# Index scores one by one with dense pieces between them, and two gate tiles moved ahead of the second forgetting pair, in a hybrid attention trunk

## The chip, the cores and the metric

The kernel runs on one core of one Trainium2 chip, in one launch. The metric is the device time of the launch in microseconds (us). Engines: PE is TensorE (matmuls), DVE is VectorE, ACT is ScalarE, POOL is GpSimd, SP is SyncE, which here issues DMAs.

## The reference

One layer of a decoder trunk on 512 tokens of width 1024, float32:

```python
x = x + token_mixer(rmsnorm(x, g1), ...)      # four causal token mixers A to D, gated, summed, @ w_out
x = x + conv_ffn(rmsnorm(x, g2), ...)         # gated MLP, width 2816, causal depthwise conv of width 3
return rmsnorm(x, g3)
```

`token_mixer` makes one projection of the normalised input and splits it into queries, keys and values of four mixers with four heads of 64 each: stick-breaking attention (S below), block-sparse attention with a T5 bias (M, "MoBA"), forgetting attention (F, "FoX") and D, attention over the 128 keys per query that an indexer selects. The indexer's score of query t and key s is a sum over 8 index heads of width 32, `sum_h w[t,h] * relu(q_idx[t,h] . k_idx[s])`, and the top 128 per row are kept. Stick-breaking needs, for each row, `log_sigmoid(-z)` and its reverse running sum, and weighs values with `exp(log_sigmoid(z) + that sum)`. Each mixer's output is multiplied with `w_branch`, gated with `sigmoid(xn @ w_gate)`, summed and multiplied with `w_out`.

## The kernel before, in words

All large products are made at about float32 precision by splitting each operand into a rounded part (hi) and a rest (lo) and adding three products (hi hi, hi lo, lo hi) in PSUM. A projection tile (128 outputs, 512 tokens, depth 1024) is thus 24 matmuls of 512 columns. `proj` (line 258) and `dense_steps` (line 114) hand them out in four pieces of six; the planner books 1.28 us for each (line 122). A values tile (VS, VM; `vgroup`, line 294) is 12 pieces of eight matmuls of 256 columns, booked at 0.85 us. After a tile's last piece its eviction follows: multiplication with the row factor on DVE (line 266), then copies and subtractions on ACT and DVE for the hi and lo parts. Each weight tile is loaded by SP (line 100), cast to hi on ACT (line 90) and subtracted to lo on POOL or DVE (line 91); three buffers of hi and lo serve all tiles in the order of the stream.

TensorE's order is written out by hand: it runs the program in the order in which the Python code emits it. The other engines' order is made by a scheduler. The mixer stage (lines 628 to 711) takes 16 heads in the order F0 F1, S0 S1, F2 F3, S2 S3, then M and D, one per "step" n = 0 to 15, and ends with steps 16 and 17. (F0q, F0k name the first forgetting *pair*, heads F0 and F1; F1q, F1k the second, heads F2 and F3; S0q to S1k in the same way.) In each step:

- `slot(n, 0, 1.5)` emits dense pieces until 1.5 us are booked; then the head's scores begin, in up to four parts (for softmax heads one block of 128 rows each, 128, 256, 384 and 512 columns wide; for S heads the matmuls `z` of four column blocks, two of them in the third part). After each part, index scores may follow (lines 703 and 704), then `slot(n, pos, ...)` with quotas of 0.5, 2, 0.5 and 1 us, then one more of 1 us (QUOTA, line 890).
- A slot first emits what falls due from earlier heads: for a softmax head, `turn` (transposes of the softmax, line 476) one step later and `pv` (line 494) two steps later, both at position 1; for an S head `weights` (line 537) one step later and `pv` two steps later, both at position 3 (LAG, line 892).
- `dense(us)` (line 609) takes the next tile of ORDER (line 885). If the tile's GATE (line 887) is a step not yet reached, it returns with nothing; it does not skip to a later tile. F1q opens in step 2, S1q in step 4, M0q in step 6. Two tiles are never in work at a time.

Index scores: 24 of them, for row blocks 3, 2 and 1 and eight heads each (line 636), in groups of three: one group after the last part of head 0, four groups in step 1, three in step 2 (IXN, line 893). Each (line 423) is one matmul of 512, 384 or 256 columns into a PSUM bank of its own, a relu on ACT and a multiply-add into the block's sum on DVE; the bank is free after that. Banks of this kind are six, shared with scores, transposes, `pv` and the z of S heads; projections have two more. When all index scores are out, DVE gets the rounds of the top-128 search (line 439), a few per slot.

The S head: after its z, ACT takes Abs (line 524), Exp (526) and Ln (527), DVE three additions (529), ACT a cast to `lh` (533), POOL the subtraction to `ll` (534). `weights` multiplies a triangle matrix with `lh` and then with `ll` (line 545), block by block, on top of z.

Of a gate tile (G0 to G7 for the first branch, H0 to H7 for the second) only the projection and one DVE multiplication are made in this stage.

Of the kernel before, what the change touches and what calls it, by code (L numbers as in the profile page):

```python
# [49 lines left out]
def trunk(ctx: ExitStack, tc: tile.TileContext, xt, wv0, wv, wp, wdk, wg, wb, wo, wu, wd,  # L50
# [79 lines left out]
    def bank(name, tag="a"):  # L130
        return psum.tile([P, S], F32, name=name, tag=tag, bufs=6 if tag == "a" else 2)
# [22 lines left out]
    stream.append((wdk, (KT, 100), V))  # L154
    order = ORDER.split()
    pidx = {"ix0": 0, "ix1": 1, "F0q": 2, "F0k": 3, "F1q": 4, "F1k": 5, "M0q": 6, "M0k": 7, "M1q": 8, "M1k": 9,
# [21 lines left out]
    with ExitStack() as ph:  # L178
# [228 lines left out]
        def bias_head(h):  # L407
            e = pp.tile([P, S], F32, name=f"e{h}", tag="e", bufs=3)
            r = bdram[h // 4][h % 4].rearrange("p y -> (p y)")
            SP.dma_start(e, r[127:127 + P * 639].rearrange("(p y) -> p y", y=639)[:, :S])  # L410
            return e
# [11 lines left out]
        def index_score(i, h):  # L423
            n = P * (i + 1)
            if h == 0:
                isc[i] = pp.tile([P, n], F32, name=f"isc{i}")
            t = isc[i]
            ps = bank(f"ip{i}{h}")[:, :n]
            T.matmul(ps, iq[h][:, i * P:(i + 1) * P], ixk[:, :n], start=True, stop=True)
            A.activation(ps, ps, AF.Relu)  # L430
            if h == 0:
                V.tensor_scalar(out=t, in0=ps, scalar1=ixw[:, i, 0:1], scalar2=None, op0=OP.mult)
            else:
                V.scalar_tensor_tensor(out=t, in0=ps, scalar=ixw[:, i, h:h + 1], in1=t, op0=OP.mult, op1=OP.add)
            if h == 7:
                G.affine_select(out=t[:, i * P:], in_=t[:, i * P:], pattern=[[-1, P]], base=0, channel_multiplier=1,
                                compare_op=OP.is_ge, fill=INADM)
# [171 lines left out]
        def dense(us):  # L609

            while us > 0 and (state["gen"] is not None or state["i"] < len(order)):
                if state["gen"] is None:
                    key = order[state["i"]]
                    if GATE.get(key, -1) > step[0]:
                        return
                    state["gen"] = dense_item(key)
                try:
                    us -= next(state["gen"])
                except StopIteration:
                    finished.add(order[state["i"]])  # L620
                    state["gen"] = None
                    state["i"] += 1

        def require(key):
            while key not in finished:
                dense(0.1)
# [30 lines left out]
        def topk(n):  # L657
            nonlocal done_topk
            for _ in range(n):
                if not done_topk and next(tk, "end") == "end":  # L660
                    done_topk = True
# [6 lines left out]
        def slot(n, pos, us):  # L668
            for st, nm in due.pop((n, pos), ()):
                if nm in "SM":  # L670
                    require("V" + nm)
                st()
            dense(us)
            if not idx:
                tkc[0] += TKS[min(n, 15)]
                while tkc[0] >= 1:
                    topk(1)
                    tkc[0] -= 1
# [3 lines left out]
        while due or n < len(heads):  # L682
            step[0] = n
            if n in BCOPY:
                i = BCOPY.index(n)
                with tc.issue_after(kdma[0].ins):
                    SP.dma_start(bdram[i], brd[4 * i:4 * i + 4].rearrange("p (o y) -> p o y", o=1).to_broadcast([4, P, 640]))
            for h in EBIAS.get(n, ()):
                with tc.issue_after(kdma[0].ins):
                    ebias[h] = bias_head(h)  # L690
            slot(n, 0, QUOTA[0])
            if n < len(heads):
                pr, nm, stages = heads[n]
                require(pr + "q")
                if nm == "D":
                    topk(100)
                else:
                    require(pr + "k")
                parts = stages[0]()
            for pos in range(1, 5):  # L700
                if n < len(heads):
                    next(parts, None)
                    for _ in range(min(len(idx), IXN[min(4 * n + pos - 1, 4)])):
                        index_score(*idx.pop(0))
                slot(n, pos, QUOTA[pos])
            if n < len(heads):
                for _ in parts:
                    pass
            slot(n, 5, QUOTA[5])
            n += 1  # L710
# [137 lines left out]
    for f in range(KT):  # L848
# [11 lines left out]
        else:  # L860
# [21 lines left out]
NV0 = 328  # L882
DCH = ((0, 8), (8, 8), (16, 6))

ORDER = ("ix0 ix1 F0q F0k S0q S0k VS F1q F1k G0 S1q S1k G1 M0q M0k VM M1q M1k G2 G3 D0q G4 G5 D1q G6 G7 "
         "H0 H1 H2 H3 H4 H5 H6 H7")
GATE = {"F1q": 2, "S1q": 4, "M0q": 6, "VM": 7, "M1q": 8, "D0q": 10, "D1q": 12, "H0": 10, "H4": 12}

# [2 lines left out]

LAG = [((1, 1), (2, 1)), ((1, 3), (2, 3))]
IXN = [0, 0, 0, 3, 3]
TKS = [1.2] * 16
EBIAS = {6: (0, 1), 8: (2,), 10: (3,), 11: (4, 5), 12: (6,), 14: (7,)}
BCOPY = (2, 5)
# [96 lines left out]
```

## Time and profile before

| what | value |
|---|---|
| time, median of 3 runs | 857.58 us (857.57 to 859.62) |
| the profiled execution's own time | 857.41 us |
| its span, first to last instruction | 855.6 us |
| PE busy | 837.3 us, 98% of the span |
| DVE busy | 538.1 us, 63% |
| ACT busy | 398.8 us, 47% |
| POOL busy | 164.6 us, 19% |
| mean granted TensorE clock | 0.996 of full |

The times of the sections below are us from the span's start. Profiled durations are to be set against 857.41 us; 1.8 us of it lie outside the span. An instruction's row has its start, its duration, engine, line, operation, what it writes and reads, its shape, how many follow one another, and in brackets the engine's idle time before it with what ended it. Matmuls overlap: one starts before the one ahead of it has ended, so the distance between two starts tells what a matmul costs.

### The profile page before, as it was taken

What the parts mean: (1) busy time and instruction counts of PE and PEld (TensorE: products, weight loads), DVE (VectorE), ACT (ScalarE), POOL (GpSimd) and SP (SyncE); (2) the same over time, 40 slices, a digit from 0 to 9 for tenths busy, and PEclk for the clock granted to TensorE, in tenths of its full rate; (3) what the DMA queues carried; (4) which work ended last, traced back from release to release, by engine and by line L of the source; (5) the groups of instructions that cost most, each with busy time, mean ns of one, the idle gap of its engine ahead of it and who ended that gap; (6) DMA issues with size and microseconds to landing.
All of it is one profiled execution on the core that took longest, in us unless ns stands there. A gap on an engine that the chain in (4) does not pass through costs nothing.

```text
span 855.6 us, 10625 instructions
## 1 busy us (share of the span) xinstructions
PE 837.3 (98%) x4019; PEld 702.2 (82%) x4019; DVE 538.1 (63%) x931; ACT 398.8 (47%) x612; POOL 164.6 (19%) x131
## 2 busy tenths in 40 slices
PE   8999999999999999999999999999999999999995
PEld 7778887888888888888888888888888888888885
DVE  5947899996453468455554477777777777333234
ACT  6556785664554843232344454444444444232231
POOL 1244575377568300000001200000000000000000
PEclk9999999999999999999999999999999999999998
DMA  6567334326332243232223223333333333333322
GB/s 227 167 163 178 100 132 108 87 58 189 90 120 74 75 130 117 74 103 96 77 74 107 89 98 98 99 99 99 98 99 99 98 97 91 90 93 93 90 65 98
DMA packets 31667, 90.68 MB, mean 106 GB/s; under 512 B 3384, under 2 KB 8376, under 8 KB 31616
## 3 DMA queue, kind: packets, MB, share of 16 engines
q1 hardware_dynamic: 30240, 88.62, 34.3%
q10 hardware_dynamic: 1376, 1.38, 0.5%
q8 instruction: 31, 0.51, 0.2%
q14 instruction: 20, 0.16, 0.1%
HBM read 83.78 MB, written 5.82 MB: 105 GB/s over the span
## 4 chain that ended last, share of the span: by engine, by line
PE 80%; DVE 1%; POOL 0%; ACT 0%; issue 0%; DVEq 0%; POOLq 0%
PE u L120 28%; PE dg L120 19%; PE dn L833 14%; PE o L120 5%; PE b L120 5%; PE vpsVM L303 1%; PE dM1q L120 1%; PE dM1k L120 1%; PE zb L545 1%; PE dD1q L120 1%; PE dD0q L120 1%; PE ptD L484 1%; PE ptM L484 1%; PE dM0q L120 0%; PE oD L500 0%; PE oM L500 0%
## 5 line engine op out<-in xcount | busy, mean ns | idle before, releaser
L90 ACT CAST wh<-wr 128x1024 fp32r<-128x1024 f32 (+1 forms) x129 | 133.7, 1039 | 153.8 <-PE dn L833 70.4
L91 DVE TENSOR_TENSOR wl<-wr,wh 128x1024 fp32r<-128x1024 f32 (+2 forms) x97 | 116.3, 1200 | 138.6 <-ACT wh L90 63.6
L120 PE MATMUL u<-xhi,wh 128*128 128x512 f32 x352 | 87.5, 390 | 0.0
L91 POOL TENSOR_TENSOR wl<-wr,wh 128x1024 fp32r<-128x1024 f32 x32 | 77.0, 2408 | 52.9 <-PE dix L120 15.3
L120 PE MATMUL u<-xlo,wh 128*128 128x512 f32 x352 | 87.1, 389 | 0.0
L120 PE MATMUL u<-xhi,wl 128*128 128x512 f32 x352 | 87.1, 389 | 0.0
L809 DVE SCALAR_TENSOR_TENSOR cv<-h,cvp,cv 128x511 f32<-128x511 f32 x88 | 66.0, 751 | 26.2 <-ACT cv L807 24.6
L120 PEld LDWEIGHTS u<-xhi,wh 128*128 128x128 f32 x352 | 66.1, 188 | 14.1 <-issue 0.5
L120 PEld LDWEIGHTS u<-xlo,wh 128*128 128x128 f32 x352 | 66.1, 188 | 13.7
L120 PEld LDWEIGHTS u<-xhi,wl 128*128 128x128 f32 x352 | 66.1, 188 | 13.7
L807 ACT ACTIVATE cv<-h,cvp 128x512 f32<-128x512 f32 x44 | 35.9, 815 | 79.8 <-DVE h L805 79.8
L833 PE MATMUL dn<-mh,wh 128*128 128x512 f32 (+1 forms) x198 | 72.9, 368 | 0.0
L833 PE MATMUL dn<-ml,wh 128*128 128x512 f32 (+1 forms) x198 | 72.3, 365 | 0.0
L833 PE MATMUL dn<-mh,wl 128*128 128x512 f32 (+1 forms) x198 | 72.3, 365 | 0.0
L120 PE MATMUL dg<-xlo,wh 128*128 128x512 f32 x256 | 66.1, 392 | 0.0
L120 PE MATMUL dg<-xhi,wh 128*128 128x512 f32 x256 | 64.9, 390 | 0.0
L120 PE MATMUL dg<-xhi,wl 128*128 128x512 f32 x256 | 64.3, 390 | 0.0
L120 PEld LDWEIGHTS dg<-xhi,wl 128*128 128x128 f32 x256 | 47.7, 188 | 9.8
L120 PEld LDWEIGHTS dg<-xhi,wh 128*128 128x128 f32 x256 | 47.8, 188 | 9.4
L120 PEld LDWEIGHTS dg<-xlo,wh 128*128 128x128 f32 x256 | 47.4, 188 | 9.5
L781 POOL TENSOR_TENSOR rstd<-rstd,sqo 128x512 f32<-128x512 f32 x7 | 9.1, 1302 | 187.1 <-ACT sqo L780 187.1
L833 PEld LDWEIGHTS dn<-ml,wh 128*128 128x128 f32 x198 | 37.3, 188 | 6.2
(430 smaller groups left out, 1453.0 us busy)
## 6 DMA issues: line engine op xcount, KB each, us to landing
wr<-in_wu SPq DMA_DIRECT2D x44, 512.0 KB
wr<-in_wg SPq DMA_DIRECT2D x32, 512.0 KB
wr<-in_wp SPq DMA_DIRECT2D x16, 512.0 KB
wr<-in_wd SPq DMA_DIRECT2D x16, 512.0 KB
wbr<-in_wb SPq DMA_DIRECT2D x8, 512.0 KB
wr<-in_wo SPq DMA_DIRECT2D x8, 512.0 KB
wr<-in_wd SPq DMA_DIRECT2D x8, 384.0 KB
bdram<-brd SPq DMA_DIRECT2D x2, 1280.0 KB
```

Source lines behind the costliest of these rows:

```text
L90: A.copy(hi, raw)
L91: eng.tensor_tensor(out=lo, in0=raw, in1=fr(hi), op=OP.subtract)
L120: T.matmul(o, a[:, k], b(k), start=(n == 0), stop=(n == len(todo) - 1))
L303: T.matmul(ps, a[:, k, ts_], b, start=(m == 0), stop=(m == 3 * KT - 1))
L484: T.transpose(pt[:, (i - j) * P:(i - j + 1) * P], z[:, QOFF[i] + P * j:QOFF[i] + P * (j + 1)], ident)
L545: T.matmul(zs[j][:, P * (j2 - j):n], trir if j2 == j else negr, x[:, KOFF[j2]:KOFF[j2] + n2], start=False, stop=(j2 == NB - 1 and x is ll) ...
L781: G.tensor_tensor(out=acc, in0=acc, in1=sq, op=OP.add)
L807: A.activation(c, h, AF.Identity, scale=cvp[:, i, 2:3], bias=cvp[:, i, 3:4])
L809: V.scalar_tensor_tensor(out=c[:, x:], in0=h[:, :S - x], scalar=cvp[:, i, 2 - x:3 - x], in1=c[:, x:], op0=OP.mult, op1=OP.add)
L833: T.matmul(o, a, b[:, k, cs], start=(n == 0 and m == 0), stop=(n == ND - 1 and m == 2))
```

## The change

After each index score, `dense(0.4)` emits one piece of dense work (a piece is the least it can emit), so a group of three scores has a piece behind each; and G0 and G1, which stood behind F1k and behind S1k, stand ahead of F1q in the order. The gates are as before. G0 and G1 have none.

```diff
                     for _ in range(min(len(idx), IXN[min(4 * n + pos - 1, 4)])):
                         index_score(*idx.pop(0))
+                        dense(IXD)
                 slot(n, pos, QUOTA[pos])
...
-ORDER = ("ix0 ix1 F0q F0k S0q S0k VS F1q F1k G0 S1q S1k G1 M0q M0k VM M1q M1k G2 G3 D0q G4 G5 D1q G6 G7 "
+ORDER = ("ix0 ix1 F0q F0k S0q S0k VS G0 G1 F1q F1k S1q S1k M0q M0k VM M1q M1k G2 G3 D0q G4 G5 D1q G6 G7 "
          "H0 H1 H2 H3 H4 H5 H6 H7")
...
 IXN = [0, 0, 0, 3, 3]
+IXD = 0.4
```

## Rows read from the trace of the kernel before

**Rows 1.** The page: engines' busy time, and POOL's costliest group (busy, mean ns).

```profile
PE 837.3 (98%) x4019; PEld 702.2 (82%) x4019; DVE 538.1 (63%) x931; ACT 398.8 (47%) x612; POOL 164.6 (19%) x131
...
L91 POOL TENSOR_TENSOR wl<-wr,wh 128x1024 fp32r<-128x1024 f32 x32 | 77.0, 2408 | 52.9 <-PE dix L120 15.3
```

**Rows 2.** Windows: length; PE, PEld, DVE, ACT, POOL busy (x); PEclk, DMA, GB/s.

```profile
350.00:450.00 100.00, 100.00 (x443) 82.81 (x442) 55.41 (x69) 34.00 (x42) 0.00 (x0) 1.00 0.29 88
```

**Rows 3.** PE's timeline, around the index scores of steps 0 and 1.

```profile
69.96 0.85 PE L429 MATMUL ip<-ixk,iq 128*128 128x512 f32 x3
70.66 1.11 PE L303 MATMUL vpsVS<-wh,xlo 128*128 128x256 f32 x8
...
79.61 0.28 PE L464 MATMUL sF<-kF0k,qF0q 128*128 128x256 f32 x1
...
86.56 2.02 PE L120 MATMUL dF1q<-xhi,wh 128*128 128x512 f32 x8
```

**Rows 4.** Waits of PE: us in total, times, longest.

```profile
PE ip L429 <- DVE stF L467: 0.6, 1, 0.6
...
PE ip L429 <- DVE isc L434: 0.4, 2, 0.2
```

**Rows 5.** Timeline of all engines, from the last z of S0 to its weights.

```profile
98.39 0.27 PE L521 MATMUL zb<-mskr,idr 128*128 128x128 f32 x1
...
99.88 0.49 ACT L524 ACTIVATE a<-zb 128x384 f32<-128x384 f32 x1
...
101.09 1.29 ACT L526 ACTIVATE a<-a 128x1280 f32<-128x1280 f32 x1
...
103.19 1.38 ACT L527 ACTIVATE a<-a,one 128x1280 f32<-128x1280 f32 x1
...
104.61 1.62 DVE L529 SCALAR_TENSOR_TENSOR a<-zb,a 128x512 f32<-128x512 f32 x3 [0.71 <-ACT a L527]
...
105.71 0.39 PE L519 MATMUL zb<-qS0q,kS0k 128*128 128x512 f32 x1
...
106.23 0.45 PE L499 MATMUL oF<-phF,vvF 128*128 128x512 f32 x1
106.32 1.26 ACT L533 CAST lh<-a 128x1280 fp32r<-128x1280 f32 x1 [1.28 <-DVE a L529]
...
107.50 1.14 PE L120 MATMUL dg<-xlo,wh 128*128 128x512 f32 x4
107.66 2.97 POOL L534 TENSOR_TENSOR ll<-a,lh 128x1280 fp32r<-128x1280 f32 x1 [1.85 <-ACT lh L533]
...
111.85 0.45 PE L545 MATMUL zb<-lh,trir 128*128 128x512 f32 x1
...
112.49 0.44 PE L545 MATMUL zb<-ll,trir 128*128 128x512 f32 x1
```

**Rows 6.** PE's timeline: F2's softmax and transposes, the last z of S2, VM.

```profile
128.37 1.07 PE L120 MATMUL dS1k<-xlo,wh 128*128 128x512 f32 x4
...
134.92 0.98 PE L484 MATMUL ptF<-cst,zF 128*128 128x128 f32 x7 [0.42 <-POOL zF L472]
...
152.63 0.27 PE L521 MATMUL zb<-mskr,idr 128*128 128x128 f32 x1
...
163.50 1.22 PE L303 MATMUL vpsVM<-wh,xhi 128*128 128x256 f32 x8 [1.30 <-DVE vvM L211]
```

**Rows 7.** POOL's timeline: the last block of F0's softmax, S2's subtraction.

```profile
72.94 1.04 POOL L472 TENSOR_TENSOR zF<-zF,stF 128x512 f32<-128x512 f32 x1 [2.05 <-DVE stF L471]
...
159.76 2.94 POOL L534 TENSOR_TENSOR ll<-a,lh 128x1280 fp32r<-128x1280 f32 x1
```

**Rows 8.** PE's timeline: its first matmuls (warming up) and its last.

```profile
1.32 4.16 PE L200 MATMUL wps<-warm 128*128 128x512 f32 x9 [1.32 <-POOL warm L186]
...
846.34 0.70 PE L840 MATMUL msf<-sqe,cst 128*128 128x256 f32 x2 [0.96 <-ACT sqe L872]
```

**Rows 9.** Windows behind the last matmul, same columns as rows 2.

```profile
848.00:850.00 2.00, 0.00 (x0) 0.00 (x0) 1.86 (x4) 0.00 (x1) 0.00 (x0) 0.59 0.00 0
```

## The prediction

> **What bounds the kernel now.** The page first: TensorE (PE) is busy for 98% of the span [rows 1]. The windows say where that is certain: between 350 and 450 us PE is busy for all 100.00 us, at the full clock [rows 2], and in the chain of waits the later stages are PE's matmuls one behind the other. Whatever is lost ahead of that stretch moves the end by as much, and whatever is saved likewise. So only the token mixer, up to about 200 us, has room, and there the PE timeline is to be read, by the starts of its instructions, because its order is written out by hand and nothing overtakes.
>
> The place that the change aims at is the index scores. Three scores of 512 columns that wait for nothing stand 0.70 us apart from the next work, 0.233 us each [rows 3]. From the scores of FOX (forgetting attention) head F1, block 1, at 79.61 to the first matmul of F1q at 86.56 PE takes 6.95 us [rows 3]. The work in it, priced by columns from that 0.70: block 1 of F1 about 0.25, three scores of up to 512 columns 0.70, a VS piece 1.1 [rows 3], block 2 about 0.35, three scores of 384 columns 0.5, block 3 about 0.45, three more scores 0.5; sum 3.85. So 3.1 us are stall: scores wait for PSUM banks, which come free when VectorE (DVE) has added the earlier ones. The list of waits puts only 0.6 and 0.4 us on these scores [rows 4]; it counts gaps between modelled ends, and the starts say 3.1. I take the starts. The Trainium skill, Trainium Kernel Development and Optimization, section Performance Expectations, warns that matmul busy time judges badly because matmuls are pipelined; this stretch agrees (1.0 us of gaps, 3.1 us by starts). By the gaps alone the gain below would be 2.1 us smaller.
>
> **The change, part by part.** I follow the planner's loops by hand with the old and the new numbers. No matmul, transfer or eviction is added or removed: the 24 scores stay, the projections stay. What changes is which work stands between which on PE.
>
> First, after each score one piece of dense work follows. In step 0 the three scores get VS pieces between them. In step 1, G0 and G1 stand next in the order, ungated, so of their eight pieces six go behind the step's first six scores and two to its quotas, and both tiles are done halfway through the step; then F1q is gated (it opens in step 2), and six scores of 384 columns come bare again, with blocks 2 and 3 of F1 among them. In step 2, F1q and F1k go wholly between the scores. Then S1q is gated until step 4.
>
> The gain: up to 3.1 us of stall goes, since a piece of six matmuls, 6 x 0.233 = 1.4 us, is longer than the DVE addition that a score waits for. The six bare scores may still wait for a bank; I leave 0.6 us there, the longer of the two waits on them [rows 4]. Gain 2.5, between 1.0 (six of the stretch's nine scores are bare, and keep 6/9 of the 3.1) and 3.1.
>
> What moves with a tile: G0 and G1 bring their weight load on SP's queue, a cast on ScalarE (ACT) and a subtraction on GpSimd (POOL), ahead of those of F1q and F1k. The tiles keep their places in the stream one for one, so a load, a cast and a subtraction of the same size stand where the others stood. I cost that at nothing; the cover is the PE work between a tile's split and its use, now more of it. Were it gone, one POOL subtraction of 2.4 us [rows 1] would show.
>
> The price: what is taken ahead is missing later. Step 3 now has no dense work at all (it had G0), nor has step 5 (it had G1), and the last three pieces of F1k no longer stand behind the scores in step 2. G0 was 24 matmuls, 24 x 0.233 = 5.6 us.
>
> Step 3 holds "weights S0", which needs the whole chain of stick-breaking head S0. Its last score matmul starts at 98.39 and ends at 98.66; then ACT takes Abs 0.49, Exp 1.29, Ln 1.38, DVE 1.62, ACT's cast 1.26, POOL's subtraction 2.97, which ends at 110.63 [rows 5]. That is 12.0 us from the last score, 9.0 us of bare work. Head S2 takes 152.90 to 162.70, 9.8 us [rows 6, 7]. Before the change PE came to the weights at 111.85 [rows 5], just when they were ready: F1k's pieces and G0 were the cover. Afterwards only this stands between: three scores of 256 columns 0.4 (half the columns of the 0.70), z of S1 block 0 0.52, pv of F1 1.27 [rows 5], the three narrower z blocks about 0.4 and 0.6, together 3.2; and the first four matmuls of the weights, which need only lh, 0.64 [rows 5]. Cover 3.9. The chain in the new place: F1q's copies, which held back Abs until 99.88 though the scores ended at 98.66 [rows 5], are done long before; that takes 1.2 off the 12.0. F1k's casts, S1's Abs and the index relus stay. I take 10.8. Stall 10.8 - 3.9 = 6.9; between 5.1 (9.0 of bare work) and 8.1 (12.0 as now).
>
> While PE waits so long its clock may fall. At the tail it is at full speed until the last matmuls at 846.34 and then falls: the mean of 848 to 850 is 0.59, on the way from 2.4 to 1.2 GHz [rows 8, 9]. Ahead of the fall PE did only these two matmuls, after a gap of 0.96 [rows 8]. At the start the nine warming matmuls take 4.16 us [rows 8], 0.46 each against 0.233: about 4 us at the low level. Waking up again costs half of that, 2.0 us. Within the mixer the clock stayed at full through a gap of 1.30 [rows 6], so those rows say nothing of 6.9 us. I take the fall, +2.0. The Trainium skill, TensorE: Matmul & The Clock Gate, section Why this matters for your kernels, says that idle gaps between bursts of matmuls bring the clock back to half rate; no stretch of this trace ahead of the tail shows it. By that rule the sum holds the 2.0, by the mixer's rows alone it would be 2.0 lower.
>
> Step 5 has "turn F2" without G1 ahead. It needs the last block of F2's softmax. F0's chain took from 69.96 to 73.98, 4.0 us [rows 3, 7]; F2's own took from 128.37 to 134.92, 6.55 us [rows 6], and PE paid 0.42 of it. New cover: S1k's last two pieces 2.8, the first block of F3 and three transposes about 0.3; 3.1. Stall 0.9 to 3.45; I take 2.0, between, because in F2's chain POOL also did a weight split, which need not fall there again. Minus 0.4: +1.6. Behind it, pv of S1 and F3's blocks come quicker than ph and pl leave their banks: +0.4, between nothing and 1.6 (DVE's pass over one head's blocks, 1.62 [rows 5], in the way).
>
> Given back later: DVE has top-k rounds in its backlog, for which PE waits, as at 163.50, 1.30 us [rows 6]. When PE stalls, DVE catches up: -0.8, between nothing and -1.3, the whole of that wait.
>
> Sum: -2.5 + 6.9 + 2.0 + 1.6 + 0.4 - 0.8 = +7.6, on the profiled execution's 857.4 us (span 855.6, 1.8 outside it), which stands 0.2 under the median of 857.58. That gives 865.0.
>
> **The rivals.**
>
> The clock stays up: everything else as above, +5.6, 863.0. For it speaks that the four lh matmuls and step 3's scores break up the wait; against it the fall at the tail, with two matmuls just ahead. Chance 0.22.
>
> The clock falls twice, or the step 5 wait is as long as F2's chain: +2.0 and more on the sum, 867 to 870. It is decided in step 5, by whether PE's wait there, too, is enough for a fall. Chance 0.13.
>
> A draw: the chain of S0 runs near its bare 9.0 us since ACT and DVE have less to do (stall 5.1), the clock stays, step 5 costs 0.5, the scores give 3.1 and DVE gives back 1.3: 5.1 + 0.5 - 3.1 - 1.3 = +1.2, 858.6. Chance 0.15.
>
> The other side, faster: the weights of S0 are not waited for, and the scores' 2.5 stay: 854.9. This decides at one point: S0's chain, last score to ll, would have to be under 3.9 + 2.5 = 6.4 us. Against it stands the sum of its rows, 9.0 us in series on three engines; for it only that the records of a busy mixer may overstate what an emptier one needs. Chance 0.08.
>
> That the change doesn't do what it says, because weights for G0 come too late, would leave PE waiting in step 1 and add to the loss; the splits have 5 us and more of PE work ahead of them, and I give it nothing of its own.
>
> **How the numbers follow.** Forecast 0.42, clock stays 0.22, worse 0.13, draw 0.15, faster 0.08. A measurement of this kernel tells some 0.3%, 2.6 us, from no change: slower 0.77, same 0.15, faster 0.08. The point is the forecast's. The range leaves out the faster case, the draw's lower half and the far end of the worse one: 858.6 to 869.5.
>
> **What would show it.** In the changed profile: the 512-column scores with a piece behind each, 1.6 us apart, and no wait on isc until the bare six. PE's longest wait then is at the second half of "weights S0" (line 545), released by POOL's ll (line 534), ACT's lh just before; some 3 us for each. A granted clock under 1.00 in the window of that wait and just behind it. A wait of "turn F2" (line 484) for POOL's z, about 2 us. From step 10 on the order is the same, and the shift against before is constant. I am wrong if weights S0 follows S1's last z block within 2 us, or if ll is done under 7 us after S0's last score; and if the clock reads 1.00 throughout, that term falls.

## The result, and the profile after

The changed kernel takes 871.67 us (median of 5 runs, 870.20 to 873.01) against 857.58 of the kernel before (5 runs beside it): ratio 1.0158, 95% interval [1.0142, 1.0174], so slower by 14 us. The forecast was 865.0 with a range of 858.6 to 869.5: the direction held, the size did not.

The page after, to stand beside [rows 1]; PEclk is the granted clock of TensorE in 40 slices, in tenths, 9 being 90% or more:

```profile
span 868.6 us, 10634 instructions
...
PE 840.5 (97%) x4019; PEld 706.2 (81%) x4019; DVE 537.9 (62%) x931; ACT 400.5 (46%) x612; POOL 164.6 (19%) x131
...
PEclk9999989999999999999999999999999999999998
```

The span grew by 13.0 us (855.6 before). Counts are the same; PE's busy time rose by 3.2 us because the same matmuls ran slower in a few places, and the rest is idle time. The list of PE's waits says what ended it (total, times, longest; the list that [rows 4] show for the kernel before):

```profile
PE ip L429 <- DVE plF L488: 4.5, 1, 4.5
PE zb L519 <- DVE oTf L503: 3.5, 2, 3.3
PE ptF L484 <- POOL zF L472: 1.9, 2, 1.2
PE zb L519 <- DVE isc L434: 1.3, 1, 1.3
...
PE oS L499 <- DVE stF L467: 1.2, 1, 1.2
...
PE vpsVM L303 <- DVE vvM L211: 0.9, 1, 0.9
```

The longest wait is one that the prediction did not have: an index score waits 4.5 us. Before asking why, it helps to see where in the mixer the time went. Six anchors on PE's timeline cut it into five stages; in the kernel before the last three are these rows (the first three are the 69.96 of [rows 3] and the 98.39 and 112.49 of [rows 5]):

```profile
114.63 0.67 PE L120 MATMUL dS1q<-xhi,wh 128*128 128x512 f32 x2
...
140.81 0.39 PE L120 MATMUL dM0q<-xhi,wh 128*128 128x512 f32 x1
...
207.17 0.39 PE L120 MATMUL dD0q<-xhi,wh 128*128 128x512 f32 x1
```

and in the changed kernel:

```profile
69.68 0.39 PE L429 MATMUL ip<-ixk,iq 128*128 128x512 f32 x1
...
116.77 0.28 PE L521 MATMUL zb<-mskr,idr 128*128 128x128 f32 x1
...
128.09 0.80 PE L545 MATMUL zb<-ll,trir 128*128 128x512 f32 x1 [0.32 <-POOL ll L534]
...
131.79 1.60 PE L120 MATMUL dS1q<-xhi,wh 128*128 128x512 f32 x6
...
154.12 2.00 PE L120 MATMUL dM0q<-xhi,wh 128*128 128x512 f32 x8
...
219.78 0.61 PE L120 MATMUL dD0q<-xhi,wh 128*128 128x512 f32 x2
```

A stage's distance minus the matmuls in it, at 0.227 us for 512 columns (443 of them fall into the 100 us of [rows 2]) and less for narrower ones (0.12 for 256, the step between their starts at full clock), is what PE lost there. Stages: A from the first index score to the last z of S0, B on to the first matmul that needs ll, C on to S1q, D on to M0q, E on to D0q. In us:

| kernel | A | B | C | D | E |
|---|---|---|---|---|---|
| before | 5.1 | 1.0 | 0.3 | 2.1 | 6.2 |
| changed | 8.8 | 7.7 | 1.9 | 3.7 | 5.5 |
| difference | +3.7 | +6.7 | +1.6 | +1.6 | -0.7 |

A is where the index scores stand (steps 0 to 2), B is step 3, D is step 5 at its end. The differences sum to 12.9 of the span's 13.0. The levels hang on the price of the transposes of 128 columns: they are counted at about 0.06 here, while their starts stand 0.11 us apart at full clock. At that price A, D and E are lower by about 0.8, 0.4 and 0.7 in every kernel, and the differences stay. Of A's +3.7, the forecast had said -2.5.

**Stage A.** ACT's timeline, between the scores of step 1:

```profile
83.27 0.58 ACT L430 ACTIVATE ip<-ip 128x512 f32<-128x512 f32 x1 [1.00 <-PE ip L429]
91.12 1.04 ACT L90 CAST wh<-wr 128x1024 fp32r<-128x1024 f32 x1 [7.27 <-DMA wr<-in_wp]
92.07 1.40 ACT L487 CAST phF<-ptF 128x512 fp32r<-128x512 f32 x4
93.34 0.62 ACT L430 ACTIVATE ip<-ip 128x512 f32<-128x512 f32 x1
```

ACT stands still for 7.27 us because the next instruction in its order is the cast of a weight tile (F1k's) that has not landed. Behind it stand turn F0's copies and the relu of the next score. PE does not need that tile until 107 us; it needs the bank that those copies empty:

```profile
87.83 1.07 PE L120 MATMUL dg<-xlo,wh 128*128 128x512 f32 x4
93.43 0.50 PE L429 MATMUL ip<-ixk,iq 128*128 128x512 f32 x1 [4.53 <-DVE plF L488]
93.77 1.80 PE L120 MATMUL dg<-xlo,wh 128*128 128x512 f32 x4
```

SP's queue says why the tile is late. The load was issued at 80.39, the copy of the bias rows (line 687, 1280 KB within DRAM) at 69.84, ahead of it in the same queue:

```profile
69.84 0.71 SPq L687 DMA_DIRECT2D bdram<-brd  x1
80.39 14.58 SPq L100 DMA_DIRECT2D wr<-in_wp  x3
```

(The second row runs together three loads, of which F1k's is the first.)

The DMA view of 74 to 92 us gives the time from issue to landing, 10.6 us:

```profile
wr<-in_wp SPq DMA_DIRECT2D x2, 512.0 KB, 10.6
```

In the kernel before that copy was issued at 70.57, the load of the tile in F1k's stream place only at 84.75, and its cast stood behind the copies of turn F1, at 94.11, with nothing waiting for it:

```profile
84.75 2.66 SPq L100 DMA_DIRECT2D wr<-in_wp  x2
```

```profile
94.11 1.05 ACT L90 CAST wh<-wr 128x1024 fp32r<-128x1024 f32 x1 [0.34 <-ACT phF L487]
```

When G0 and G1 are used up in step 1 (before the change in steps 3 and 5), the tile two places ahead in the stream is asked for earlier too, and its cast moves to the front of turn F0's copies.

**Stage B** went as forecast in size. PE's timeline, step 3:

```profile
119.20 0.50 PE L519 MATMUL zb<-qS0q,kS0k 128*128 128x512 f32 x1 [1.34 <-DVE isc L434]
...
125.05 0.58 PE L519 MATMUL zb<-qS0q,kS0k 128*128 128x256 f32 x1 [3.32 <-DVE oTf L503]
...
126.18 0.41 PE L521 MATMUL zb<-mskr,idr 128*128 128x128 f32 x1
126.39 0.73 PE L545 MATMUL zb<-lh,trir 128*128 128x512 f32 x1
```

and POOL's end of S0's chain:

```profile
125.11 2.93 POOL L534 TENSOR_TENSOR ll<-a,lh 128x1280 fp32r<-128x1280 f32 x1 [4.19 <-ACT lh L533]
```

From the start of S0's last z at 116.77 to the end of ll at 128.04 the chain takes 11.3 us (11.0 when counted from that matmul's end, as the forecast's 10.8 is), and the matmuls under it come to 3.6 (forecast 3.9). The loss is the difference; only its place is another. PE never gets to stand 6.9 us at weights S0, since the z blocks of S1 ahead of them wait first, for a bank of an index score and for the bank of pv F1, whose addition on DVE stands behind S0's own 1.62 us and a step of the top-128 search there.

**Stage C** is the clock. Windows (length; PE, PEld, DVE, ACT, POOL busy; PEclk, DMA share, GB/s):

```profile
94.00:97.00 3.00, 3.00 (x9) 2.33 (x8) 2.29 (x7) 2.25 (x5) 1.52 (x3) 0.50 0.36 94
...
125.00:128.00 3.00, 2.72 (x10) 2.43 (x10) 2.83 (x5) 1.36 (x3) 2.89 (x1) 0.50 0.26 102
128.00:131.00 3.00, 2.91 (x11) 2.82 (x12) 2.93 (x7) 2.27 (x3) 0.04 (x1) 0.50 0.29 108
```

So 1.2 GHz in two places, behind the gap of 4.53 us in step 1 and behind that of 3.32 in step 3 (0.50 is the lower of the clock's two levels). The prediction weighed the Trainium skill, TensorE: Matmul & The Clock Gate, section Why this matters for your kernels (idle gaps between bursts bring the clock back to half rate): the changed kernel's trace agrees, 0.50 after both gaps, where the kernel before showed nothing of it in the mixer.

### The profile page after: what moved, and what is told of

Same layout as the page of the kernel before. It is cut to its first block, busy times and chain, and to the rows that moved or that the text cites. A ratio compares the mean times of both kernels' runs of the same rounds, so it can differ in the third digit from the quotient of the medians.

```text
span 868.6 us, 10634 instructions
## 1 busy us (share of the span) xinstructions
PE 840.5 (97%) x4019; PEld 706.2 (81%) x4019; DVE 537.9 (62%) x931; ACT 400.5 (46%) x612; POOL 164.6 (19%) x131
## 4 chain that ended last, share of the span: by engine, by line
PE 85%; DVE 9%; ACT 2%; DMA 2%; issue 1%; POOL 0%; SPq 0%; DVEq 0%; ACTq 0%; POOLq 0%
PE u L120 28%; PE dg L120 19%; PE dn L834 14%; PE o L120 5%; PE b L120 5%; DVE isc L446 2%; DVE m L445 1%; PE vpsVS L303 1%; DMA wr<-in_wp 1%; PE vpsVM L303 1%; DMA xr<-in_xt 1%; PE dF0k L120 1%; PE dM1q L120 1%; PE zb L545 1%; PE dF1q L120 1%
## 5 line engine op out<-in xcount | busy, mean ns | idle before, releaser
L120 PEld LDWEIGHTS dg<-xhi,wl 128*128 128x128 f32 x256 | 48.6, 191 | 10.1
L834 PEld LDWEIGHTS dn<-mh,wh 128*128 128x128 f32 x198 | 37.3, 188 | 6.2
```

Of the source, the lines that this page charges most:

```text
L120: T.matmul(o, a[:, k], b(k), start=(n == 0), stop=(n == len(todo) - 1))
L834: T.matmul(o, a, b[:, k, cs], start=(n == 0 and m == 0), stop=(n == ND - 1 and m == 2))
```

## The experiments

Losses by stage of every kernel run, as above. "Chain" is S0's, from the start of its last z to the end of ll, and "cover" the matmuls between that last z and the first that needs ll, priced at full clock (e7's with its fill).

| kernel | us | ratio, 95% interval | A | B | C | D | E | chain, cover |
|---|---|---|---|---|---|---|---|---|
| e1 | 865.69 | 1.0096 [1.0081, 1.0111] | 6.6 | 5.2 | 2.2 | 3.2 | 6.4 | 10.1, 4.9 |
| e2 | 861.76 | 1.0049 [1.0034, 1.0064] | 3.0 | 0.7 | 0.3 | 6.9 | 7.3 | 10.6, 13.1 |
| e3 | 865.05 | 1.0087 [1.0072, 1.0102] | 2.4 | 7.7 | 2.2 | 4.3 | 5.5 | 11.3, 3.6 |
| e4 | 869.08 | 1.0140 [1.0123, 1.0157] | 6.1 | 7.7 | 2.2 | 3.8 | 5.5 | 11.3, 3.6 |
| e5 | 874.75 | 1.0197 [1.0183, 1.0211] | 10.1 | 4.7 | 2.2 | 9.1 | 4.9 | 12.4, 7.6 |
| e7 | 866.28 | 1.0096 [1.0082, 1.0110] | 2.4 | 4.7 | 0.5 | 5.9 | 6.7 | 11.3, 7.6 |
| e8 | 862.43 | 1.0050 [1.0036, 1.0063] | 10.3 | 1.0 | 0.3 | 2.1 | 6.6 | 12.2, 13.1 |
| e9 | 857.68 | 1.0003 [0.9994, 1.0011] | 5.1 | 1.0 | 0.3 | 2.1 | 6.2 | 12.2, 13.1 |
| e10 | 867.05 | 1.0109 [1.0095, 1.0124] | 3.4 | 4.7 | 2.2 | 7.6 | 5.9 | 12.4, 7.6 |
| e11 | 856.23 | 0.9982 [0.9973, 0.9991] | 3.5 | 1.0 | 0.3 | 2.1 | 6.7 | 12.2, 13.1 |
| e12 | 855.35 | 0.9971 [0.9960, 0.9983] | 3.1 | 1.0 | 0.3 | 2.1 | 6.2 | 12.2, 13.1 |
| e13 | 860.74 | 1.0035 [1.0021, 1.0048] | 3.0 | 0.7 | 0.3 | 4.4 | 8.1 | 10.5, 13.1 |

**The two halves of the change alone.** e1 has only the pieces between scores, on the order before; e2 only the new order.

```diff
 e1:  ORDER as before
 e2: -IXD = 0.4
     +IXD = 0.0
```

> The piece behind each index score alone, with the old order of tiles (G0 behind F1k, G1 behind S1k). Theory: two separate losses. In step 1 nothing ungated is left, so the scores stand bare there and the late load of a weight tile has no cast in front of turn F0's copies: no wait of 4.5 us and no fall of the clock near 90 us. In step 2 the pieces use up F1q, F1k and G0, so step 3 is empty as with the whole change, and its loss of about 8 us (waits before the z of S1 and weights S0, with a fall of the clock) is there in full; step 5 keeps G1. Expected 857.6 + 8 = 865.5 us. Rival: the loss is mainly in step 1 and comes from the pieces between the scores; then this kernel, which has none in step 1, is within 2 us of the kernel before.

> The new order of tiles alone, no piece behind a score. Theory: G0 and G1 are taken by the quotas of steps 1 and 2, so F1q and F1k move back into steps 2 and 3 and cover the wait for weights S0 as G0 did; step 5 is empty and costs 1.5 to 2 us at turn F2 and pv of S1. Expected 859 us, clock 1.00 up to the tail. Rival: moving the weight loads is what costs; then the wait of ACT for a late load shows here too, and the time is 862 us or more.

e1 came out as expected, e2 2.8 us above. Neither half wins alone, and not for one reason. e1 spends VS on the first scores and leaves step 1 bare (A rises by 1.5, the clock is at 0.57 from 83 to 87 us), and F1k's pieces leave step 3, so B and C are lost. In e2 step 3 keeps F1k and loses nothing, and the scores of step 1 gain 2.1 us (A); its loss is step 5 (D, +4.8), where turn F2 waits 3.1 us, and 1.1 us behind it (E).

**The late weights.** e3 makes the two copies of the bias rows later (steps 3 and 8 for 2 and 5), nothing else; e4 leaves the copies and puts F1k's cast behind turn F0's copies on ACT; e9 is the control, the kernel before with later copies. (The edits of e4 and of e13 below are shortened.)

```diff
 e3 (on the changed kernel):
-BCOPY = (2, 5)
+BCOPY = (3, 8)
 e4 (on the changed kernel), in split_weight for F1k's tile:
-        A.copy(hi, raw)
+        with tc.issue_after(turned[-1]):   # the last ph copy of turn F0
+            A.copy(hi, raw)
 e9 (on the kernel before):
-BCOPY = (2, 5)
+BCOPY = (4, 8)
```

> The changed kernel with the first of the two bias copies in DRAM issued from step 3 on, the second from step 8 (they were at 2 and 5). Theory: the copy takes a part of the DMA engines from 75 to 89 us, so that F1k's weights, asked for at 80.4 us, land at 91.0; ACT, which has F1k's cast next in its queue, stands still, and PE waits 4.5 us for a bank and then runs at the low clock. With the copy out of the way the load lands in about 4 us, the wait and the fall go, and 4.7 + 1.7 us come off: 865.3 us. The loss of step 3 stays. Rival: the wait before the second score of step 1's second group belongs to turn F0 and the banks, not to the load; then it stays, 871 us.

> The changed kernel with one cast moved four places back on ACT: F1k's, from ahead of turn F0's four copies to behind them. Loads and the DRAM copy are as in the changed kernel. Theory: the load is as late as before (91 us), but the copies and so the banks no longer wait for it; most of the 4.5 us and the fall of the clock at 94 us go: 865 to 867 us. Rival: what delays PE is the traffic of the DMA engines itself or the banks; then 871 us.

> The kernel before with one edit: the bias rows are copied in steps 4 and 8 instead of 2 and 5, so that the first copy no longer runs while the weights of F1q and F1k are loaded. Theory (the copy delays the load in the kernel before too, but there the cast waiting for it stands behind turn F0's copies, so nothing on TensorE waits): no difference, 857 to 858. Rival (the stall of the scores in step 1 of the kernel before is itself partly that load): 854 to 856, and then the change's gain that was forecast was partly the copy's.

e3 is 6.6 us faster than the changed kernel, and A falls from 8.8 to 2.4. Its DMA view of the same stretch and its ACT timeline show the load at its usual time and the cast with 0.33 us of waiting:

```profile
wr<-in_wp SPq DMA_DIRECT2D x3, 512.0 KB, 3.7
```

```profile
84.92 1.05 ACT L90 CAST wh<-wr 128x1024 fp32r<-128x1024 f32 x1 [0.33 <-DMA wr<-in_wp]
85.88 1.40 ACT L487 CAST phF<-ptF 128x512 fp32r<-128x512 f32 x4
```

e4 missed its expectation (865 to 867): the 4.5 us wait is gone, but ACT still stops for 3.64 us at the cast, the relus behind it are late, PE waits for them in shorter pieces, and the clock falls a little later all the same (0.67 from 95 to 98 us). Moving the late cast behind one user handed more than half of the loss to the next (A 6.1, against 8.8 in the changed kernel and 2.4 in e3), while e3's earlier landing removed it. e9 shows that the copy by itself costs nothing (ratio 1.0003): in the kernel before no cast that anything waits for falls into its time. The 4.5 us belong to the pair of them.

**The cover of S0's chain.** e5 was to bring F1k's three pieces back behind the last z of S0; its copy, however, was tied to an earlier load and ran at 71 us again, so A spoils it. e10 is the same with the copy late.

```diff
 e5 (on e3):
-                        dense(IXD)
+                        if n < 2:
+                            dense(IXD)
 e10 (on e5):
-BCOPY = (3, 8)
+BCOPY = (4, 8)
```

> The changed kernel with the copy of the bias rows moved to steps 3 and 8 (as in e3) and the piece behind each score kept in steps 0 and 1 only, so that F1k's last three pieces stand behind the last block of S0 again. Theory (step 3 loses because the cover of S0's chain is gone, and the clock falls because of that): cover 3.9 + 4.2 = 8.1 us against a chain of 11.0, so one wait of about 2.9 us at the second half of weights S0, none at the z blocks of S1, the granted clock 1.00 throughout; of e3's 10.3 us of excess between 100 and 125 us about 4 stay: 859 to 860. Rival (the two empty steps cost what they cost wherever F1's pieces stand): about what the order alone gave, 861.8, with the waits at turn F2 and at VM of that run. Second rival (the loss is the bare scores' banks in step 2): 865 as in e3.

> e5 again, with the copy in step 4 instead of 3. In e5 F1k ends only in step 3, so the copy was still bound to S0k's load and ran at 71 us, beside the loads it was to leave alone; the 4.7 us wait in step 1 and the lower clock were there again, and e5 tells nothing of step 3. Theory (cover): 4.7 of wait and some 1.7 of low clock go, no further fall of the clock in step 3, 861 to 863, about what the order alone gave. Rival (step 3 loses in its bare scores, whatever stands behind S0): the waits of e5 of 2.8 and 0.9 us at 121 and 126 us stay and the clock falls in step 3 again: 866 to 869.

By the time, e10 sides with the rival (867.05). The stages say something else. B is chain minus cover wherever the cover is shorter: 11.3 - 3.6 in the changed kernel, e3 and e4, 10.1 - 4.9 in e1, 12.4 - 7.6 in e5 and e10, within 0.1 us each; where the cover is 13.1, B is at most 1.0. (As B is counted, that follows whenever the first matmul on ll starts as ll ends. That it does start so, within 0.1 us, in these six kernels is what the runs show. In e7 the fill itself ended later.) So the theory of B holds, but the expected wait of 2.9 us was too small (the chain is 12.4 there, not 11.0), the clock falls as well, and step 5 takes 7.6 instead of the 3.7 of the changed kernel. The expectation left out that last term, which e2 had already shown.

**The clock.** e7 fills e3's waits with matmuls that nothing needs, to hold the clock up; `filler(c)` issues c of 512 columns into one bank that nothing reads.

```diff
 e7 (on e3), n == 3: ahead of z S1.0 and z S1.2, and ahead of the ll part of weights S0
+                    filler(5 if pos == 1 else 7)
+                        if h == 0 and j == 0 and x is ll:
+                            filler(6)
```

> e3 with 18 more matmuls of 512 columns in step 3 whose result nothing reads (5 ahead of the first block of S1, 7 ahead of its third, 6 ahead of the part of weights S0 that needs ll): 18 x 0.227 = 4.1 us of extra work at the full clock, put where e3 waits 1.34, 1.80 and 1.49 us. They fill waits and shorten none. Theory (the two stretches at the lower clock cost a share of their own beside the waits): the clock stays at 1.00 through step 3, its matmuls run at the full rate, and the time falls by 2 to 3 us against e3's 865.05, to 862 to 863. Rival (the chains of S0 and of pv F1 set when step 3 ends, and a faster clock only lengthens the waits): 865 again, clock up. Second rival (the fill overlaps no wait): 865 to 869.

The time did not fall (866.28 against 865.05), which lies in the second rival's 865 to 869. With the fill the clock still drops (0.65 from 119 to 122 us), but earlier and for less of the work that counts: e7's PE timeline passes from the first matmul on ll to S1q in 2.29 us, against 4.01 in e3 (122.39 to 126.40).

```profile
120.25 2.87 PE L662 MATMUL fill<-ixk,idr 128*128 128x512 f32 x6
122.91 0.59 PE L547 MATMUL zb<-ll,trir 128*128 128x512 f32 x1
...
125.20 2.06 PE L120 MATMUL dS1q<-xhi,wh 128*128 128x512 f32 x8
```

So the fall in C costs 1.7 us (2.2 against 0.5), and only for the matmuls behind the release. In e3 the clock is down ahead of ll too (0.75 from 116 to 119 us), and that costs nothing, since the chain ends when it ends. e7 paid its gain back: the fill ended 1.2 us after ll (ll was ready at 121.73), and D rose by 1.6, E by 1.2.

**Step 5.** D is 2.1 with a tile in step 5 (3.2 in e1), and without one either 3.7 to 4.3 (the changed kernel, e3, e4) or 5.9 to 9.1 (e2, e5, e7, e10; e5's 9.1 has a further fall of the clock in it, 0.50 from 155 to 159 us). In each of the second group turn F2 waits 3.1 us. PE's and POOL's timelines of e2:

```profile
138.17 0.98 PE L484 MATMUL ptF<-cst,zF 128*128 128x128 f32 x7 [3.09 <-POOL zF L472]
```

```profile
131.84 2.97 POOL L553 TENSOR_TENSOR wl<-w,wh 128x1280 fp32r<-128x1280 f32 x1 [0.25 <-PE sF L465]
134.76 2.35 POOL L91 TENSOR_TENSOR wl<-wr,wh 128x1024 fp32r<-128x1024 f32 x1
137.07 1.04 POOL L472 TENSOR_TENSOR zF<-zF,stF 128x512 f32<-128x512 f32 x1
```

The last softmax block of F2 stands behind a weight split, and so it does in e5, e7 and e10. In the changed kernel, as in e3 and e4, it stands ahead of it:

```profile
148.50 1.03 POOL L472 TENSOR_TENSOR zF<-zF,stF 128x512 f32<-128x512 f32 x1
149.50 2.37 POOL L91 TENSOR_TENSOR wl<-wr,wh 128x1024 fp32r<-128x1024 f32 x1
```

e13 is e2 with these two swapped.

```diff
 e13 (on e2), in split_weight for one tile (stream place 17):
-        eng.tensor_tensor(out=lo, in0=raw, in1=fr(hi), op=OP.subtract)
+        with tc.issue_after(zmul["F2"]):   # F2's last multiplication on POOL
+            eng.tensor_tensor(out=lo, in0=raw, in1=fr(hi), op=OP.subtract)
```

> The order alone (e2) with one swap on GpSimd: the 2.4 us subtraction that splits one weight tile stands behind the multiplication of F2's last softmax block instead of ahead of it. In e2 that subtraction ran from 134.76 to 137.11 and the multiplication came behind it at 137.07, and turn F2 waited 3.1 us; where the multiplication stands first (the changed kernel, e3) the wait is 0.8 to 1.1. Theory (the place of that split decides the empty step 5): the wait falls to about 0.8, the 6.9 us lost between S1q and M0q become 4.5 to 5, 859.3 to 860.0. Rival (the wait moves on to pv of S1, released by pl of F2 on VectorE, 1.5 us in e2, which needs the same VectorE backlog either way): 861 to 862.

D falls from 6.9 to 4.4 and turn F2's wait to 0.9, as the theory had it; E gives 0.8 of it back (a wait of 1.8 us for a softmax block of M, also on POOL), and the median gains 1.0 instead of 2, which misses the theory's 860.0 (runs from 858.72 to 861.40). PE's timeline in e13 (its lines stand three later):

```profile
136.04 0.98 PE L487 MATMUL ptF<-cst,zF 128*128 128x128 f32 x7 [0.88 <-POOL zF L475]
138.79 0.47 PE L502 MATMUL oS<-wh,vvS 128*128 128x512 f32 x1 [1.19 <-DVE stF L470]
```

**A version that keeps the gain.** If A's 2 to 3 us are real and the losses are the emptied steps, then steps 3 and 5 must get another tile. e8 and e11 do that with the change's pieces; e12 without pieces bound to scores and with one tile only.

```diff
 e8 (on e5):
-... VS G0 G1 F1q F1k S1q S1k M0q M0k VM M1q M1k G2 G3 D0q G4 G5 D1q G6 G7
+... VS G0 G1 F1q F1k G2 S1q S1k G3 M0q M0k VM M1q M1k G4 G5 D0q G6 G7 D1q
-                slot(n, pos, QUOTA[pos])
+                slot(n, pos, 1.2 if n > 8 and pos == 2 else QUOTA[pos])
 e11 (on e8):
-BCOPY = (3, 8)
+BCOPY = (4, 8)
 e12 (on the kernel before):
-... VS F1q F1k G0 S1q S1k G1 M0q M0k VM M1q M1k G2 G3 D0q G4 G5 D1q G6 G7
+... VS G0 F1q F1k G1 S1q S1k G2 M0q M0k VM M1q M1k G3 G4 D0q G5 G6 D1q G7
-BCOPY = (2, 5)
+BCOPY = (4, 8)
```

> A version meant to beat both: the change's G0 and G1 between the scores of steps 0 and 1, but the steps 3 and 5 get G2 and G3 in their place, the two tiles missing later are spread over steps 9 to 16 (quota of position 2 there 1.2 instead of 2), pieces behind scores in steps 0 and 1 only, bias rows copied in steps 3 and 8. Theory (the stall of the scores in step 1 is worth some 3 us, and the change loses only through the two steps it empties and the late weights): no clock fall, weights S0 and turn F2 wait no longer than before, 854 to 855, ratio 0.996 to 0.997. Rival (steps 9 to 16 lack the two tiles as steps 3 and 5 did, waits for the top-k on VectorE grow there): 857 to 859.

> e8 again, with the copy in step 4. e8 had one large wait left, the 4.1 us in step 1 with the clock at 0.50 behind it; its excess between 75 and 100 us was 7.5 us, against 1.1 in e3 where the copy ran late. Theory (late weights): 862.43 - 6.4 = 856.0, ratio about 0.998, and 854.5 if the step 1 wait had also made the 1.4 us wait of turn F1. Rival (the wait in step 1 is not the copy's but the cast's place): 862 again.

> The kernel before with the copy in step 4, no piece bound to a score, and only G0 ahead of F1q; the later gate tiles move up one place (G1 into step 3, G2 into step 5), and the one missing lies between steps 9 and 16. So nothing is emptied, and G0's four pieces stand at the quotas of step 1's second half, between its groups of three bare scores. Theory (the stall there is DVE's pace, filled by 5.6 us of work that TensorE owes anyway): 2 to 3 us of it go, 854.5 to 856. Rival (steps 9 to 16 wait for the top-k instead): 857 to 858.

e8 missed because of its early copy (A 10.3); e11, with the copy late, is at 856.23 where 856.0 was expected: 1.1 us faster than the kernel before (857.38 beside it), with the change's pieces in steps 0 and 1 and its G0 and G1 in their new places. e12 is the best of all: 855.35, 2.0 us faster than the kernel before and 16 faster than the changed one. Its page and its waits:

```profile
span 853.6 us, 10633 instructions
...
PE 837.7 (98%) x4019; PEld 704.1 (82%) x4019; DVE 538.3 (63%) x931; ACT 398.8 (47%) x612; POOL 164.7 (19%) x131
```

```profile
PE vpsVM L303 <- DVE vvM L211: 1.3, 1, 1.3
PE ptF L484 <- POOL zF L472: 1.1, 2, 0.7
```

B, C, D and E read as before the change, and A has lost 2.0 us. The pieces bound to scores are not needed: four pieces of G0 at the ordinary quotas do as much for A (3.1) as the spread ones of e11 (3.5). Whether e12 needs its later copy was not tried.

## Why the prediction went wrong in size

**The index scores, -2.5.** The size is right once nothing else stands in the way: A goes from 5.1 to 2.4 in e3, a gain of 2.7, and to 3.0 to 3.5 in e2, e10, e11 and e12. That dense work in step 1 fills the stall is right too, but it need not stand behind each score: the order alone (e2) gains 2.1 of the 2.7. In the changed kernel the term came out as +3.7.

**What moves with a tile, "I cost that at nothing".** This is the step that failed, and it holds nearly the whole miss: 871.67 - 865.05 = 6.6 us between the changed kernel and e3. The cover named there was "the PE work between a tile's split and its use", and that cover was there: F1k is used at 107 us, its cast ended at 92.2. But a cast that waits for its load also stops what stands behind it on ACT, here the copies of turn F0, on which PE waits at once: 4.53 us, and some 1.7 more at the lower clock behind it. And the load came 4.4 us earlier (80.39 against 84.75), further into the time of another transfer on SP's queue, the copy of the bias rows, which the prediction never priced. Places in the stream were kept one for one, as it says; the times were not. Both queues had to be followed for the tile two places ahead in the stream, not only for the tiles named in the diff. The rival "weights for G0 come too late" was close, but the tile was F1k's, and it was given nothing of its own on the same wrong ground.

**Weights S0, +6.9.** Measured +6.7 (B), from a chain of 11.3 and a cover of 3.6. That is a loss of 7.7 where 6.9 was forecast; it comes out nearer because the kernel before already lost 1.0 there, which the prediction took as nothing ("just when they were ready"). The prediction put the wait at the second half of weights S0, some 3 us for each of lh and ll; it fell at the z blocks of S1 instead, 1.34 and 3.32 us, with 0.32 left for ll. By its own sign ("weights S0 follows S1's last z block within 2 us") it was wrong on the place: 0.21 us lie between the two starts. The sum of a chain less its cover does not depend on which instruction meets the wait.

**The clock, +2.0.** Measured 1.6 in stage C, as forecast. A second fall in step 1, which the late weights brought, was not in the forecast; the slow matmuls between 94 and 97 us account for some 1.7 of A.

**Step 5, +1.6 and +0.4; given back, -0.8.** Measured +1.6 in all of D, and -0.7 in E. That D came out near the forecast was partly luck of the order on POOL: the same empty step costs 4.8 us (6.9 against 2.1) where a weight split stands ahead of F2's last block. The reason given for the lower wait ("POOL also did a weight split, which need not fall there again") was the right question without a look at the answer.

With A as forecast the terms measured in e3 are -2.7, +6.7, +1.9, +2.2 and -0.7, together 7.4, and 865.05 against the forecast's 865.0. One term put at nothing carried the time out of the range.

**The rivals.** "The clock stays up" and the draw fell with the 0.50 of the windows and the chain of 11.3 us; "faster" asked for a chain under 6.4. The case "the clock falls twice" (867 to 870) did occur, but in step 1, not in step 5.

## What to carry to other kernels

Before a weight tile is moved, follow its load and its cast as queue entries: ask what the load queues behind and what waits behind the cast on its engine, for every tile that is fetched ahead because of the move, not only whether PE has the data in time. Price a wait as chain less cover, with both counted between the same two instructions; where the cover is work that is owed anyway, give the emptied place another tile and not just the place that gains. Before emptying a step, look at which of two neighbours comes first on an engine off the critical path: a 2.4 us instruction ahead of a 1 us one decided 2.5 us of PE's time in step 5 here, of which 1.0 was left in the median.

## What the runs showed of the hardware

A load of 512 KB took 10.6 us from issue to landing beside the copy within DRAM, and 3.7 without it, though the DMA engines were far from busy on the mean. The DMA view of 75 to 91 us in the changed kernel (busy share of the 16 engines in 40 slices, tenths), and below it e3's:

```profile
DMA  9743322222222223975987795985222222222222
```

```profile
DMA  9976110000000000026499559589300000009289
```

Two tenths is the copy alone, 102 GB/s. From 86.6 to 88 us nothing else ran (packets, MB, share of 16 engines):

```profile
q1 hardware_dynamic: 56, 0.14, 25.5%
```

That fits the Trainium skill, DMA: Bandwidth & Descriptors, section Why a DMA increments its semaphore by 16 and not by 1: the number of DMA engines a transfer uses follows from its outer dimensions, here four, and a transfer has landed only when its last engine is through. By that rule the load's share on the copy's four engines is what came late. The share of a quarter agrees, and so do the sizes of the packets in the changed kernel's trace: the copy's are of 2560 bytes and run from 75.8 to 89.4 us; of the 256 packets of 4096 bytes of F1k's load and the next one, 192 start by 86.2 us and the other 64, a quarter, from 88.6 to 91.8. The runs do not name the engine of each packet, and a copy spread over more engines was not tried.

A fall of the clock does not always cost time: matmuls that run at 1.2 GHz under a chain that ends later cost nothing (B is the chain less the cover at full clock, also where the windows show 0.50 in it). Nor does the longest gap alone tell where it falls: in e2 a wait of 3.1 us in step 5 passed with the clock at 1.00 in the window from 125 to 150 us, where one of 3.32 in the changed kernel's step 3 was followed by 0.50, and in e1 the clock read 0.57 from 83 to 87 us behind gaps of at most 0.56 us. What tells these apart was not tried.
